# One core: 64 of the dense tokens take their expert activations from gathered rows

## The chip, the cores and the metric

One NeuronCore of a Trainium2 chip runs the whole layer in one launch. The metric is device time in microseconds. The engines are TensorE (PE in the rows, with its weight loads as PEld), VectorE (DVE), ScalarE (ACT), GpSimd (POOL, which here issues the indirect gathers) and SyncE (SP, which issues most loads).

## The reference

One encoder block: adaLN, a mixer, a residual, and then a channel sub-layer that this change is about. In it each token retrieves, for each of 8 heads, 16 of 16,384 single-neuron experts (product keys), and gets their weighted sum:

```python
idx = jnp.take_along_axis(cand_i, best_pos, axis=-1)     # [tokens, 8, 16]
g = jax.nn.softmax(best_s, axis=-1)
u_sel = expert_u[idx]
act = jax.nn.gelu(jnp.einsum('phkd,pd->phk', u_sel, xb), approximate=False)
coef = (g * act.astype(jnp.float32)).astype(xb.dtype)
return jnp.einsum('phk,phkd->pd', coef, expert_v[idx])
```

There are 512 tokens of width 1024; everything is float32.

## The kernel before

The first 128 tokens are **sparse**: for each of their 128 (head, rank) pairs GpSimd gathers one row of `expert_u` per token (`gath`, 128 rows of 4 KB, 0.524 MB a gather), VectorE multiplies it with the token and sums (`dots`, tile `scr`). Later the same is done with `expert_v` (`sums`, tile `ys`). That makes 128 + 128 gathers, each with one VectorE instruction of 128x1024.

The other 384 tokens are **dense**: all 16,384 experts are computed for them as 128 chunks of 128 experts, and a gate tensor `Gd`, zero where a token did not choose an expert, picks out the chosen ones.

After a prologue (norms, mixer, queries, scores) come two stages:

* **Activation stage.** `u_chunk(c)`: 24 matmuls with 384 columns (`mm3`: 8 blocks of the width, three products each of weights and tokens split in a high and a low part), then a Gelu. `split_w` makes the high part on ScalarE (`whi`) and the low part on VectorE (`wlo`), once a chunk. Between chunks a generator, `background_E`, is drawn on: the first top-16 (`stage1`), `topk_tile` for each of four 128-token tiles, and `gates_tile` for the three dense ones. A gate step makes one-hot tiles `jh` and `igh` for four tokens, four float32 matmuls (`ps_gt`) and a copy to `stg`; every fourth step a 1 MB store to `Gd`. What is drawn is set by nominal costs: each chunk adds `STEP_E` to one budget for the background, and `STEP_ED` to one for `dots`. Activations that don't fit the ring of 32 are spilled to `Ad`.
* **Output stage.** `v_chunk`: 18 matmuls with 512 columns into six accumulators. `v_load` brings the weights, every eighth chunk three 512 KB pieces of gates (`gt`), and spilled activations. `v_coef` makes the coefficients: `cf` = activation x gate (VectorE), `ch` its high part (ScalarE), `cl` the rest (VectorE). `cf` has one buffer, `ch` and `cl` three, the split weights four. u chunks that the activation stage had no time for run here too, one beside each v chunk. The sparse work is drawn by a third budget with the factor `F_P`, and what is left after the last chunk is done at once.

The scheduling layer (`tc`) then orders each engine's instructions; each engine runs its own list strictly in order. So does each DMA queue's issuing engine.

Of the kernel before, what the change touches and what calls it, by code (L numbers as in the profile page):

```python
# [8 lines left out]
F32 = mybir.dt.float32  # L9
# [25 lines left out]
def block_kernel(ctx, tc, xT, small, w_ada1, w_ada, b_ada, w_in, w_r, w_i, w_out, w_q, keys, uT, u, v, final_g, out):  # L35
# [11 lines left out]

# [1 line left out]
    small_sb = const.tile([128, NSMALL], F32, name="small_sb")  # L49
# [67 lines left out]

# [1 line left out]
    adx = ExitStack()  # L119
# [150 lines left out]

# [1 line left out]
    mix = mx.enter_context(tc.tile_pool(name="mix", bufs=1))  # L272
# [98 lines left out]

# [1 line left out]
    pst = psA.tile([128, NT], F32, name="ps_col")  # L373
# [17 lines left out]
    nc.vector.scalar_tensor_tensor(A2, adac[:, 32:40], 1.0, sm("n2g"), op0=OP.add, op1=OP.mult)  # L391
    h2n = persist.tile([128, D], F32, name="h2n")

    def full2(k, f):
        if k % 4 == 0:
            tp_cur[0] = psZ.tile([128, 4, 128], F32, name="ps_g", bufs=2)
        nc.tensor.transpose(tp_cur[0][:, k % 4, :], f[:, 0:128], ident)
        if k % 4 == 3:
            nc.scalar.activation(h2n[:, (k - 3) * 128:(k + 1) * 128], tp_cur[0], AF.Copy)

    tp_cur = [None]
    qraw = {0: load_w(w_q[0]), 1: load_w(w_q[1])}
# [4 lines left out]

# [1 line left out]
    ep = ExitStack()  # L409
    sel = ctx.enter_context(tc.tile_pool(name="sel", bufs=1, side="right"))  # L410
    ring = ctx.enter_context(tc.tile_pool(name="ring", bufs=1, side="right"))
# [58 lines left out]

# [84 lines left out]

    def gates_tile(t):
        for gq in range(8):
            stg = stgp[0].tile([128, 128, 16], F32, name="stg", bufs=2)
            for q4 in range(4):
                t0 = gq * 16 + q4 * 4  # L560
                jh = topk.tile([128, 4, 128], F32, name="jh", bufs=2)
                nc.vector.tensor_tensor(jh, iota[:, None, :].to_broadcast([128, 4, 128]),  # L562
                                        selT[t][:, 1, t0:t0 + 4, None].to_broadcast([128, 4, 128]), op=OP.is_equal)
                ig = topk.tile([128, 4, 128], F32, name="igh", bufs=2)
                for k in range(4):
                    col = lambda n: selT[t][:, n, t0 + k:t0 + k + 1]
                    if k < ACT_OH:
# [11 lines left out]
                yield 600 + 236 * (4 - ACT_OH)  # L579

# [21 lines left out]
    def background_E():  # L602
# [15 lines left out]

    def gath(table, idxs, k):
        if k < 128 and k not in rows:  # L620
# [3 lines left out]
            rows[k] = r  # L624

    def dots():
        for k in range(128):
            for kk in range(k, k + (rows_pool[1] - 1 if rows_pool[2] else 1)):
                gath(u, idx_s, kk)
            scr = rows_pool[0].tile([128, D], F16, name="scr")  # L630
            with tc.issue_after(anchor[0]):
                nc.vector.scalar_tensor_tensor(scr, rows.pop(k), 1.0, h2n, op0=OP.mult, op1=OP.mult,  # L632
                                               accum_out=acts[:, k:k + 1])
            yield 1135

    def sums():
        nc.scalar.activation(acts, acts, AF.Gelu)
        nc.vector.tensor_mul(acts, acts, g_s)
        for k in range(128):
            for kk in range(k, k + rows_pool[1] - 1):  # L640
                gath(v, idx_s, kk)
            with tc.issue_after(anchor[0]):
# [5 lines left out]

# [1 line left out]
    hd = lambda k: h2h[:, k, 128:]  # L650
    ld = lambda k: h2l[:, k, 128:]
    uraw = {}
# [11 lines left out]
    act = {}  # L664
    Ad = dram.tile([NE, 128, ND], F32, name="Ad")

# [20 lines left out]
    while not done and c < NE:
        u_load(c + UE + 1)
        u_split(c + UE)
        u_chunk(c, psE, 2)  # L690
        if c >= RB - 4:
            spill(c - RB + 4)
        if sready:
# [4 lines left out]
        while budget > 0:  # L698
# [4 lines left out]
            budget -= n  # L703
        c += 1
    for _ in range(XE):
        u_load(c + UE + 1)
        u_split(c + UE)
        u_chunk(c, psE, 2)
        if c >= RB - 4:
            spill(c - RB + 4)  # L710
        c += 1
    rows_pool[2] = False
# [4 lines left out]

# [1 line left out]
    vp = ctx.enter_context(tc.tile_pool(name="vp", bufs=2, reuse_waits="tile"))  # L719
# [8 lines left out]
    def v_load(n):  # L728
# [95 lines left out]

# [1 line left out]
    x1s = []  # L826
# [92 lines left out]
```

## Time and profile before

| | |
|---|---|
| three runs | 1482.51, 1483.49 (median), 1487.41 us |
| span of the profiled execution | 1481.2 us |
| busy in that span: TensorE, VectorE, ScalarE, GpSimd | 1434.8, 1228.9, 679.6, 303.9 us |
| moved by DMA | 406.51 MB, 274 GB/s over the span |

The span is the time from the first to the last instruction of one profiled execution; the median of the runs lies 2.25 us above it. Busy shares are averages over stages with different limits, so what a change in one stage is worth has to be read in that stage.

### The profile page before, as it was taken

Reading aid. Unit: us, or ns where it says so; the run is one execution under the profiler, and the core shown is the slowest. Engines: PE = TensorE matmul, PEld = TensorE weight load, DVE = VectorE, ACT = ScalarE, POOL = GpSimd, SP = SyncE. Lnnn points to the kernel's source line nnn. Section 1 sums busy time; section 2 is a strip of 40 time slices with the busy share of each in tenths; the row PEclk is TensorE's granted clock in tenths of the full one; section 3 lists DMA queues with packets and bytes.
Section 4 is the critical chain, followed back from the end, with each engine's and each line's share of the span. In section 5 each row is a group of like instructions: output and inputs, shape, how many; then the busy total and the mean of one; then the engine's idle time right before and its main releaser. Section 6 shows DMA issues by size and latency. Waiting matters only on the chain.

```text
span 1481.2 us, 21793 instructions
## 1 busy us (share of the span) xinstructions
PE 1434.8 (97%) x7705; PEld 1256.8 (85%) x7705; DVE 1228.9 (83%) x2501; ACT 679.6 (46%) x1033; POOL 303.9 (21%) x270
## 2 busy tenths in 40 slices
PE   5999998989999999999999999999999999999997
PEld 2666787788999999999999989999888888888885
DVE  6775646999999999978888778788888888888887
ACT  3554434432336567656777633333333333333333
POOL 0000000000133232232222244444222222222200
PEclk9999998999999999999999999999999999999999
DMA  9566231245679988999888799899999999999881
GB/s 383 201 248 213 86 100 57 86 127 146 224 223 366 317 314 305 345 324 326 282 281 285 276 376 347 297 354 323 387 340 366 346 349 337 348 332 320 303 281 57
DMA packets 165312, 406.51 MB, mean 274 GB/s; under 512 B 14674, under 2 KB 84306, under 8 KB 160084
## 3 DMA queue, kind: packets, MB, share of 16 engines
q1 hardware_dynamic: 112724, 227.90, 44.8%
q0 software_dynamic: 37504, 136.33, 25.9%
q10 hardware_dynamic: 14976, 40.90, 7.3%
q8 instruction: 60, 0.98, 0.3%
q14 instruction: 48, 0.39, 0.1%
HBM read 359.99 MB, written 45.09 MB: 273 GB/s over the span
## 4 chain that ended last, share of the span: by engine, by line
PE 66%; DMA 1%; DVE 1%; ACT 0%; issue 0%; DVEq 0%; SPq 0%
PE acc L765 12%; PE acc L769 12%; PE acc L767 12%; PE ps_act L84 8%; PE ps_act L85 8%; PE ps_act L86 8%; PE ps_gt L575 6%; DMA gt<-Gd 1%; DMA Gd<-stg 1%; DVE rows L846 0%; PE acc L777 0%; PE acc L775 0%; PE acc L776 0%; ACT stg L576 0%; DVE rows L839 0%; DVE rows L838 0%
## 5 line engine op out<-in xcount | busy, mean ns | idle before, releaser
L75 ACT ACTIVATE whi<-wraw 128x1024 fp32r<-128x1024 f32 x292 | 307.7, 1054 | 336.9 <-PE ps_act L85 184.5
L76 DVE TENSOR_TENSOR wlo<-wraw,whi 128x1024 fp32r<-128x1024 f32 x292 | 356.3, 1220 | 64.1 <-ACT whi L75 60.2
L86 PE MATMUL ps_act<-h2h,wlo 128*128 128x384 f32 x1024 | 344.7, 337 | 7.8 <-DVE wlo L76 7.8
L84 PE MATMUL ps_act<-h2h,whi 128*128 128x384 f32 x1024 | 349.2, 341 | 1.3 <-ACT sc L465 1.2
L85 PE MATMUL ps_act<-h2l,whi 128*128 128x384 f32 x1024 | 343.1, 335 | 0.0
L622 POOL DMA_INDIRECT rows<-in_u_dram,idx_s x128 | 162.1, 1267 | 451.1 <-DVE scr L632 278.4
L765 PE MATMUL acc<-whi,ch 128*128 128x512 f32 x750 | 231.8, 390 | 3.5 <-ACT ch L756 3.5
L767 PE MATMUL acc<-wlo,ch 128*128 128x512 f32 x750 | 231.8, 390 | 0.0
L769 PE MATMUL acc<-whi,cl 128*128 128x512 f32 x750 | 231.7, 390 | 0.0
L622 POOL DMA_INDIRECT rows<-in_v_dram,idx_s x128 | 136.5, 1067 | 361.4 <-DVE ys L646 337.4
L756 ACT ACTIVATE ch<-cf 128x384 fp32r<-128x384 f32 x128 | 67.1, 525 | 310.6 <-DVE ys L646 234.4
L86 PEld LDWEIGHTS ps_act<-h2h,wlo 128*128 128x128 f32 x1024 | 192.2, 188 | 12.5 <-DVE wlo L76 12.5
L84 PEld LDWEIGHTS ps_act<-h2h,whi 128*128 128x128 f32 x1024 | 192.4, 188 | 3.0 <-ACT sc L465 1.4
L85 PEld LDWEIGHTS ps_act<-h2l,whi 128*128 128x128 f32 x1024 | 192.5, 188 | 0.8
L765 PEld LDWEIGHTS acc<-whi,ch 128*128 128x128 f32 x750 | 140.7, 188 | 31.8 <-ACT ch L756 3.8
L769 PEld LDWEIGHTS acc<-whi,cl 128*128 128x128 f32 x750 | 141.2, 188 | 29.7 <-DVE cl L757 0.3
L767 PEld LDWEIGHTS acc<-wlo,ch 128*128 128x128 f32 x750 | 141.1, 188 | 29.7
L646 DVE SCALAR_TENSOR_TENSOR ys<-rows,acts,ys 128x1024 f32<-128x1024 f32 x127 | 162.6, 1280 | 0.7
L632 DVE SCALAR_TENSOR_TENSOR scr<-rows,h2n 128x1024 f16<-128x1024 f32 x128 | 156.3, 1221 | 3.6 <-DMA rows<-in_u_dram,idx_s 2.9
L757 DVE TENSOR_TENSOR cl<-cf,ch 128x384 fp32r<-128x384 f32 x128 | 71.4, 558 | 88.7 <-ACT ch L756 85.9
L576 ACT ACTIVATE stg<-ps_gt 128x512 f32<-128x512 f32 x96 | 102.3, 1082 | 5.7 <-PE ps_gt L575 3.9
L575 PE MATMUL ps_gt<-igh,jh 128*128 128x128 f32 x768 | 96.0, 275 | 3.1 <-DVE jh L562 3.1
(229 smaller groups left out, 1662.3 us busy)
## 6 DMA issues: line engine op xcount, KB each, us to landing
wraw<-in_uT_dram SPq DMA_DIRECT2D x128, 512.0 KB
wraw<-in_v_dram SPq DMA_DIRECT2D x128, 512.0 KB
Gd<-stg ACTq DMA_DIRECT2D x24, 1024.0 KB
gt<-Gd SPq DMA_DIRECT2D x48, 512.0 KB
wada<-in_w_ada_dram SPq DMA_DIRECT2D x16, 1024.0 KB
Ad<-act ACTq DMA_DIRECT2D x80, 192.0 KB
act<-Ad SPq DMA_DIRECT2D x80, 192.0 KB
wraw<-in_w_in_dram SPq DMA_DIRECT2D x20, 512.0 KB
```

Source lines behind the costliest of these rows:

```text
L75: nc.scalar.activation(hi, raw, AF.Copy)
L76: anchor[0] = nc.vector.tensor_sub(lo, raw, hi.bitcast(F32)).ins
L84: nc.tensor.matmul(ps, hi[:, k, :], xh(k), start=first and k == ks[0], stop=False)
L85: nc.tensor.matmul(ps, hi[:, k, :], xl(k), start=False, stop=False)
L86: nc.tensor.matmul(ps, lo[:, k, :], xh(k), start=False, stop=last and k == ks[-1])
L575: nc.tensor.matmul(pg[:, k, :], jh[:, k, :], ig[:, k, :], start=True, stop=True)
L622: nc.gpsimd.indirect_dma_start(out=r[:, :], out_offset=None, in_=table, in_offset=bass.IndirectOffsetOnAxis(ap=idxs[:, k:k + 1], axis=0))
L632: nc.vector.scalar_tensor_tensor(scr, rows.pop(k), 1.0, h2n, op0=OP.mult, op1=OP.mult, accum_out=acts[:, k:k + 1])
L646: nc.vector.scalar_tensor_tensor(ys, rows.pop(k), acts[:, k:k + 1], ys, op0=OP.mult, op1=OP.add)
L765: nc.tensor.matmul(accs[b][e], ch[:, bs], hi[:, e * 512:(e + 1) * 512], start=st, stop=False)
L767: nc.tensor.matmul(accs[b][e], ch[:, bs], lo[:, e * 512:(e + 1) * 512], start=False, stop=False)
L769: nc.tensor.matmul(accs[b][e], cl[:, bs], hi[:, e * 512:(e + 1) * 512], start=False, stop=en)
```

## The change

Tokens 128 to 191 (the first half of dense tile 1, `XB` = 64) leave the dense activation product: it has 320 columns now. Their activations come from gathered rows, 64 tokens on each half of the partitions, so that 64 gathers and 64 VectorE instructions serve 64 tokens x 128 pairs. The first 64 steps of `dots` are theirs. `coef_b` puts Gelu on these activations, brings them to the layout of the gates with one matmul, and multiplies them into the gates, so that for these tokens `Gd` holds gate x activation. Their 16 gate steps move to the end of the background, and there all four one-hot tiles of a step are made on VectorE, where ScalarE had made one of four. In `v_coef` ScalarE copies those 64 columns from the gates to `cf`, and VectorE multiplies the other 320. `full2` also transposes the 64 tokens (two matmuls a block). The three budgets have new numbers.

```diff
+            for dst, src in zip((h2n, h2b), tp_cur):
+                nc.scalar.activation(dst[:, (k - 3) * 128:(k + 1) * 128], src, AF.Copy)
...
+    NU = ND - XB
...
+            if t == 1:
+                nc.scalar.activation(selB[:, 0:2, :], pt[:, 0:2, 0:XB], AF.Copy)
+                nc.scalar.activation(gTb, pt[:, 2, 0:XB], AF.Copy)
+                nc.vector.scalar_tensor_tensor(ij[:, 0], ij[:, 0], 128.0, ij[:, 1], op0=OP.mult, op1=OP.add)
+                idf = ij[:, 0].rearrange("p h k -> p (h k)")
+                for e in range(2):
+                    nc.vector.tensor_copy(idx_b[XB * e:XB * (e + 1), :], idf[0:XB, XB * e:XB * (e + 1)])
...
+        yield from topk_tile(1)
+        sready.append(1)
         yield from topk_tile(0)
-        sready.append(1)
-        yield from topk_tile(1)
-        yield from merge(gates_tile(1), topk_tile(2), 0.48)
-        yield from merge(gates_tile(2), topk_tile(3), 0.48)
-        yield from gates_tile(3)
+        yield from merge(gates_tile(1, range(4, 8), selT[1]), topk_tile(2), 0.32)
+        yield from merge(gates_tile(2, range(8), selT[2]), topk_tile(3), 0.48)
+        yield from gates_tile(3, range(8), selT[3])
+        while len(bdone) < XB:
+            yield next(dot_gen)
+        coef_b()
+        yield from gates_tile(1, range(4), selB, 0)
...
+    def coef_b():
+        for e in range(2):
+            es = slice(XB * e, XB * (e + 1))
+            nc.scalar.activation(act_p[es, es], act_b[es, :], AF.Gelu)
+        pt = psE.tile([128, 4, 128], F32, name="ps_t")
+        nc.tensor.matmul(pt[:, 0, 0:XB], act_p, sel2, start=True, stop=True)
+        nc.vector.tensor_mul(selB[:, 2, :], pt[:, 0, 0:XB], gTb)
...
+    usteps = [(idx_b, h2b, act_b, k) for k in range(XB)] + [(idx_s, h2n, acts, k) for k in range(128)]
...
-    hd = lambda k: h2h[:, k, 128:]
-    ld = lambda k: h2l[:, k, 128:]
+    hd = lambda k: h2h[:, k, T - NU:]
+    ld = lambda k: h2l[:, k, T - NU:]
...
-        nc.vector.tensor_mul(cf.rearrange("p (g t) -> p g t", t=16),
-                             act.pop(vorder[n]).rearrange("p (g t) -> p g t", t=16), gbuf.pop(n))
+        g = gbuf.pop(n)
+        nb = XB // 16
+        nc.scalar.activation(cf[:, 0:XB].rearrange("p (g t) -> p g t", t=16), g[:, 0:nb], AF.Copy)
+        nc.vector.tensor_mul(cf[:, XB:].rearrange("p (g t) -> p g t", t=16),
+                             act.pop(vorder[n]).rearrange("p (g t) -> p g t", t=16), g[:, nb:])
...
+XB = 64
 ACT_OH = 1
-STEP_E = 2450
-STEP_ED = 1400
+STEP_E = 2070
+STEP_ED = 1180
 GB_E = 4
 GB_P = 7
-F_P = 0.81
+F_P = 0.96
```

The new budgets move instructions on every engine. On TensorE all 128 u chunks now stand in the activation stage (106 before), three of them behind the last gate step (four before); the output stage is 128 v chunks and nothing else. Of the 192 dot products 104 stand in the activation stage (103 of 128 before) and 88 in the output stage, with 96 of the 128 `ys` steps.

ScalarE in the output stage, before (`ch` for one chunk, `whi` for a later one):

```order
L756 ACTIVATE ch_11511<-cf_11509 128x384
L75 ACTIVATE whi_11470<-wraw_11431 128x1024
L756 ACTIVATE ch_11546<-cf_11544 128x384
L75 ACTIVATE whi_11505<-wraw_11466 128x1024
L756 ACTIVATE ch_11585<-cf_11583 128x384
```

and with the change:

```order
L799 ACTIVATE ch_13168<-cf_13165 128x384
L77 ACTIVATE whi_13161<-wraw_13121 128x1024
L794 ACTIVATE cf_13204<-gt_12969 128x64
L799 ACTIVATE ch_13207<-cf_13204 128x384
L794 ACTIVATE cf_13240<-gt_12969 128x64
L77 ACTIVATE whi_13200<-wraw_13157 128x1024
L799 ACTIVATE ch_13243<-cf_13240 128x384
```

The new copy into `cf` stands behind the `whi` of its chunk in 40 chunks, and ahead of it in 81; since `cf` has one buffer, it can't start before the `cl` of the chunk before has read it.

VectorE at the same place, before:

```order
L757 TENSOR_TENSOR cl_11512<-cf_11509,ch_11511 128x384
L752 TENSOR_TENSOR cf_11544<-act_11433,gt_11289 128x384
L76 TENSOR_TENSOR wlo_11471<-wraw_11431,whi_11470 128x1024
L646 SCALAR_TENSOR_TENSOR ys_8675<-rows_11323,acts_2587,ys_8675 128x1024
L757 TENSOR_TENSOR cl_11547<-cf_11544,ch_11546 128x384
```

and with the change:

```order
L800 TENSOR_TENSOR cl_13169<-cf_13165,ch_13168 128x384
L795 TENSOR_TENSOR cf_13204<-act_13084,gt_12969 128x320
L78 TENSOR_TENSOR wlo_13162<-wraw_13121,whi_13161 128x1024
L684 SCALAR_TENSOR_TENSOR ys_9393<-rows_13043,acts_2613,ys_9393 128x1024
L800 TENSOR_TENSOR cl_13208<-cf_13204,ch_13207 128x384
L684 SCALAR_TENSOR_TENSOR ys_9393<-rows_13079,acts_2613,ys_9393 128x1024
L795 TENSOR_TENSOR cf_13240<-act_13123,gt_12969 128x320
L78 TENSOR_TENSOR wlo_13201<-wraw_13157,whi_13200 128x1024
```

A row (`scr` or `ys`) stands between `wlo` and `cl` of nearly every chunk; in 53 chunks a second one stands between `cl` and `cf`.

VectorE at the end of the program, before:

```order
L757 TENSOR_TENSOR cl_13846<-cf_13843,ch_13845 128x384
L752 TENSOR_TENSOR cf_13849<-act_13785,gt_13552 128x384
L757 TENSOR_TENSOR cl_13852<-cf_13849,ch_13851 128x384
L838 TENSOR_TENSOR rows_13908<-acc00_8665,gt_13855 128x512
L839 TENSOR_TENSOR rows_13908<-rows_13908,rows_13862 128x512
```

and with the change (buffer numbers left out, as equal rows then merge):

```order
L795 TENSOR_TENSOR cf<-act,gt 128x320
L684 SCALAR_TENSOR_TENSOR ys<-rows,acts,ys 128x1024
L800 TENSOR_TENSOR cl<-cf,ch 128x384
L684 SCALAR_TENSOR_TENSOR ys<-rows,acts,ys 128x1024 x32
L881 TENSOR_TENSOR rows<-acc_9380,gt 128x512
L881 TENSOR_TENSOR ys<-ys,gt 128x512 x2
```

Now 32 `ys` steps stand between the last coefficients and the closing arithmetic of all four tiles, where there was nothing, and the closing of tile 0 (`ys`) stood further up.

## Rows read from the trace of the kernel before

**Rows 1.** The page, part 1: engines' busy time, share of the span, instructions.
```profile
PE 1434.8 (97%) x7705; PEld 1256.8 (85%) x7705; DVE 1228.9 (83%) x2501; ACT 679.6 (46%) x1033; POOL 303.9 (21%) x270
```

**Rows 2.** The page, part 4: the chain that ended last, by line.
```profile
PE acc L765 12%; PE acc L769 12%; PE acc L767 12%; PE ps_act L84 8%; PE ps_act L85 8%; PE ps_act L86 8%; PE ps_gt L575 6%; DMA gt<-Gd 1%; DMA Gd<-stg 1%; DVE rows L846 0%; PE acc L777 0%; PE acc L775 0%; PE acc L776 0%; ACT stg L576 0%; DVE
```

**Rows 3.** Windows: busy us per engine, PEclk, DMA share, GB/s.
```profile
262.00:423.00 161.00, 152.24 (x873) 139.60 (x872) 160.84 (x764) 59.46 (x85) 8.84 (x10) 1.00 0.47 148
423.00:600.00 177.00, 172.62 (x1079) 171.21 (x1078) 173.72 (x364) 106.50 (x178) 58.75 (x46) 1.00 0.91 317
600.00:840.00 240.00, 240.00 (x1561) 239.97 (x1560) 206.50 (x410) 163.64 (x280) 66.38 (x53) 1.00 0.87 303
840.00:862.00 22.00, 19.09 (x116) 18.77 (x114) 9.68 (x14) 7.61 (x10) 8.72 (x8) 1.00 0.91 314
...
1035.00:1441.00 406.00, 406.00 (x1793) 336.28 (x1792) 337.46 (x394) 147.31 (x199) 83.45 (x88) 1.00 0.96 339
```

**Rows 4.** The chain in order of time: start, us, what.
```profile
829.58 0.89 PE ps_gt L575 x8
834.66 1.78 PE ps_gt L575 x16
```

**Rows 5.** Timeline of VectorE in the activation stage: start, us, what.
```profile
722.71 1.22 DVE L76 TENSOR_TENSOR wlo<-wraw,whi 128x1024 fp32r<-128x1024 f32 x1
723.85 1.22 DVE L632 SCALAR_TENSOR_TENSOR scr<-rows,h2n 128x1024 f16<-128x1024 f32 x1
...
724.99 0.69 DVE L562 TENSOR_TENSOR jh<-iota,selT 128x512 f32<-128x512 f32 x1
725.60 0.95 DVE L572 TENSOR_SCALAR igh<-iota,selT 128x128 f32<-128x128 f32 x3
726.36 0.69 DVE L562 TENSOR_TENSOR jh<-iota,selT 128x512 f32<-128x512 f32 x1
```

**Rows 6.** Timeline in the output stage, one chunk of ScalarE and VectorE.
```profile
1103.72 0.53 ACT L756 ACTIVATE ch<-cf 128x384 fp32r<-128x384 f32 x1 [2.60 <-DVE ys L646]
...
1104.15 1.04 ACT L75 ACTIVATE whi<-wraw 128x1024 fp32r<-128x1024 f32 x1
...
1104.27 0.56 DVE L757 TENSOR_TENSOR cl<-cf,ch 128x384 fp32r<-128x384 f32 x1 [0.60 <-ACT ch L756]
...
1104.87 0.56 DVE L752 TENSOR_TENSOR cf<-act,gt 128x384 f32<-128x384 f32 x1
...
1105.34 1.22 DVE L76 TENSOR_TENSOR wlo<-wraw,whi 128x1024 fp32r<-128x1024 f32 x1
...
1106.48 1.28 DVE L646 SCALAR_TENSOR_TENSOR ys<-rows,acts,ys 128x1024 f32<-128x1024 f32 x1
...
1107.80 0.53 ACT L756 ACTIVATE ch<-cf 128x384 fp32r<-128x384 f32 x1 [2.60 <-DVE ys L646]
```

**Rows 7.** Windows: a stretch of the output stage.
```profile
1040.00:1080.00 40.00, 40.00 (x178) 33.15 (x177) 33.68 (x40) 14.08 (x20) 8.96 (x10) 1.00 1.05 392
```

**Rows 8.** The chain from the last gates to the first coefficients.
```profile
841.93 1.88 ACT stg L576 x2
843.83 7.52 DMA Gd<-stg
851.41 9.91 DMA gt<-Gd
861.44 0.57 DVE cf L752
```

**Rows 9.** Timeline of VectorE: the first dot product of the sparse tokens.
```profile
423.41 1.23 DVE L632 SCALAR_TENSOR_TENSOR scr<-rows,h2n 128x1024 f16<-128x1024 f32 x1
```

**Rows 10.** Timeline of VectorE at the program's end.
```profile
1459.23 0.56 DVE L757 TENSOR_TENSOR cl<-cf,ch 128x384 fp32r<-128x384 f32 x1 [0.85 <-ACT ch L756]
1461.12 0.69 DVE L838 TENSOR_TENSOR rows<-acc,gt 128x512 f32<-128x512 f32 x1 [1.33 <-PE acc L777]
...
1476.81 1.42 DVE L846 SCALAR_TENSOR_TENSOR rows<-rows,rs,gt 128x512 f32<-128x512 f32 x2
```

More of the change, by code (lines that the diff above doesn't have):

```diff
@@ L62, in block_kernel @@
         nc.vector.memset(hind[64 * s:64 * s + 64, s:s + 1], 1.0)
+    sel2 = const.tile([128, XB], F32, name="sel2")
+    nc.vector.tensor_add(sel2, ident[:, 0:XB], ident[:, XB:2 * XB])
     h2h = persist.tile([128, KB, T], FR, name="h2h")
@@ L392, in block_kernel @@
     h2n = persist.tile([128, D], F32, name="h2n")
+    sel = ctx.enter_context(tc.tile_pool(name="sel", bufs=1, side="right"))
+    h2b = sel.tile([128, D], F32, name="h2b")
     def full2(k, f):
         if k % 4 == 0:
-            tp_cur[0] = psZ.tile([128, 4, 128], F32, name="ps_g", bufs=2)
+            tp_cur[:] = [psZ.tile([128, 4, 128], F32, name="ps_g", bufs=2) for _ in range(2)]
         nc.tensor.transpose(tp_cur[0][:, k % 4, :], f[:, 0:128], ident)
+        for e in range(2):
+            nc.tensor.matmul(tp_cur[1][XB * e:XB * (e + 1), k % 4, :], f[:, 128:128 + XB], ident, start=True, stop=True)
         if k % 4 == 3:
-            nc.scalar.activation(h2n[:, (k - 3) * 128:(k + 1) * 128], tp_cur[0], AF.Copy)
-    tp_cur = [None]
+            for dst, src in zip((h2n, h2b), tp_cur):
+                nc.scalar.activation(dst[:, (k - 3) * 128:(k + 1) * 128], src, AF.Copy)
+    tp_cur = []
     qraw = {0: load_w(w_q[0]), 1: load_w(w_q[1])}
@@ L409, in block_kernel @@
     ep = ExitStack()
-    sel = ctx.enter_context(tc.tile_pool(name="sel", bufs=1, side="right"))
     ring = ctx.enter_context(tc.tile_pool(name="ring", bufs=1, side="right"))
@@ L487, in block_kernel @@
     selT = {}
+    idx_b = sel.tile([128, XB], I32, name="idx_b")
+    selB = sel.tile([128, 3, XB], F32, name="selB")
+    gTb = sel.tile([128, XB], F32, name="gTb")
     def topk_tile(t):
@@ L553, in topk_tile, with gates_tile @@
             nc.scalar.activation(selT[t][:, 3:5, :], pt[:, 0:4:2, :], AF.Copy, scale=-1.0)
+            if t == 1:
[5 more added lines that the diff above has]
+                    nc.vector.tensor_copy(idx_b[XB * e:XB * (e + 1), :], idf[0:XB, XB * e:XB * (e + 1)])
         yield 300
-    def gates_tile(t):
-        for gq in range(8):
+    def gates_tile(t, groups, sl, aoh=None):
+        aoh = ACT_OH if aoh is None else aoh
+        for gq in groups:
             stg = stgp[0].tile([128, 128, 16], F32, name="stg", bufs=2)
@@ L578, in gates_tile @@
                     nc.scalar.dma_start(Gd[t][gq], stg)
-                yield 600 + 236 * (4 - ACT_OH)
+                yield 600 + 236 * (4 - aoh)
     stgp = []
@@ L607, in background_E, with gath @@
         stgp.append(ep.enter_context(tc.tile_pool(name="stgp", bufs=1, side="right")))
+        yield from topk_tile(1)
+        sready.append(1)
         yield from topk_tile(0)
-        sready.append(1)
-        yield from topk_tile(1)
-        yield from merge(gates_tile(1), topk_tile(2), 0.48)
-        yield from merge(gates_tile(2), topk_tile(3), 0.48)
-        yield from gates_tile(3)
-    acts = sel.tile([128, 128], F32, name="acts")
+        yield from merge(gates_tile(1, range(4, 8), selT[1]), topk_tile(2), 0.32)
[5 more added lines that the diff above has]
+        yield from gates_tile(1, range(4), selB, 0)
+    acts = sel.tile([128, 128], F32, name="acts")
+    act_b = sel.tile([128, XB], F32, name="act_b")
+    act_p = sel.tile([128, 2 * XB], F32, name="act_p")
+    nc.vector.memset(act_p, 0.0)
+    bdone = []
+    def coef_b():
+        for e in range(2):
+            es = slice(XB * e, XB * (e + 1))
[3 more added lines that the diff above has]
+        nc.vector.tensor_mul(selB[:, 2, :], pt[:, 0, 0:XB], gTb)
     rows = {}
     rows_pool = [topk, GB_E, True]
-    def gath(table, idxs, k):
-        if k < 128 and k not in rows:
+    def gath(table, idxs, k, key):
+        if key not in rows:
             r = rows_pool[0].tile([128, D], F32, name="rows", bufs=rows_pool[1])
@@ L623, in gath @@
                                          in_offset=bass.IndirectOffsetOnAxis(ap=idxs[:, k:k + 1], axis=0))
-            rows[k] = r
+            rows[key] = r
+    usteps = [(idx_b, h2b, act_b, k) for k in range(XB)] + [(idx_s, h2n, acts, k) for k in range(128)]
     def dots():
-        for k in range(128):
-            for kk in range(k, k + (rows_pool[1] - 1 if rows_pool[2] else 1)):
-                gath(u, idx_s, kk)
+        for n, (_, hn, dst, k) in enumerate(usteps):
+            for m in range(n, min(n + (rows_pool[1] - 1 if rows_pool[2] else 1), len(usteps))):
+                gath(u, usteps[m][0], usteps[m][3], m)
             scr = rows_pool[0].tile([128, D], F16, name="scr")
             with tc.issue_after(anchor[0]):
-                nc.vector.scalar_tensor_tensor(scr, rows.pop(k), 1.0, h2n, op0=OP.mult, op1=OP.mult,
-                                               accum_out=acts[:, k:k + 1])
+                nc.vector.scalar_tensor_tensor(scr, rows.pop(n), 1.0, hn, op0=OP.mult, op1=OP.mult,
+                                               accum_out=dst[:, k:k + 1])
+            bdone.append(n)
             yield 1135
@@ L639, in sums @@
         for k in range(128):
-            for kk in range(k, k + rows_pool[1] - 1):
-                gath(v, idx_s, kk)
+            for kk in range(k, min(k + rows_pool[1] - 1, 128)):
+                gath(v, idx_s, kk, kk)
             with tc.issue_after(anchor[0]):
@@ L664, in block_kernel @@
     act = {}
-    Ad = dram.tile([NE, 128, ND], F32, name="Ad")
+    Ad = dram.tile([NE, 128, NU], F32, name="Ad")
     def spill(c):
@@ L672, in u_chunk @@
         hi, lo = usp.pop(c)
-        ps = pool.tile([128, ND], F32, name="ps_act", bufs=bufs)
+        ps = pool.tile([128, NU], F32, name="ps_act", bufs=bufs)
         mm3(ps, hi, lo, hd, ld, range(KB), True, True)
-        act[c] = ring.tile([128, ND], F32, name="act", bufs=RB)
+        act[c] = ring.tile([128, NU], F32, name="act", bufs=RB)
         act_anchor[0] = nc.scalar.activation(act[c], ps, AF.Gelu).ins
@@ L680, in block_kernel @@
     budget = bd_ = 0.0
-    c = 0
     done = False
@@ L686, in block_kernel, with u_step @@
         u_split(j)
[L687 to L692, printed above, removed]
+    def u_step():
+        i = cn[0]
+        u_load(i + UE + 1)
+        u_split(i + UE)
+        u_chunk(i, psE, 2)
+        if i >= RB - 4:
+            spill(i - RB + 4)
+        cn[0] += 1
+    cn = [0]
+    while not done:
+        if cn[0] < NE:
+            u_step()
         if sready:
@@ L703, in block_kernel @@
             budget -= n
-        c += 1
     for _ in range(XE):
[L706 to L711, printed above, removed]
+        if cn[0] < NE:
+            u_step()
+    c = cn[0]
     rows_pool[2] = False
@@ L739, in v_load @@
         if act[cc] is None:
-            act[cc] = ring.tile([128, ND], F32, name="act", bufs=RB)
+            act[cc] = ring.tile([128, NU], F32, name="act", bufs=RB)
             nc.sync.dma_start(act[cc], Ad[cc])
```

6 lines of the change are left out of this document (3 added, 3 removed).

## The prediction

> **What bounds the kernel now.** I began with the page: TensorE is busy 97% of the span, VectorE 83% [rows 1]. The chain that ended last says the same: two thirds of it are matmuls, in thirds of the output product, the u product and the gates [rows 2]. Then windows by stage [rows 3]. Until 423 us VectorE is full (160.84 of 161) and TensorE loses 9. From 423 to 600 both are nearly full (TensorE loses 4.4). From 600 on TensorE has no gap and VectorE 14% of slack, in the output stage 17%. So TensorE sets the time, and the engine right behind it is VectorE; the change takes work from the first and gives work to the second, so I count both, stage by stage. DMA is the third to watch: its share is 0.96 in the output stage.
>
> **Prices.** Between two groups of gate records (829.58 + 0.89 and 834.66) lies one u chunk of 4.19 us [rows 4], 24 matmuls of 384 columns at 0.175 us. An output chunk takes 4.08 us (two `ch` apart, [rows 6]), 18 matmuls of 512 columns at 0.227. So 128 columns cost 0.052 us, 64 half of that: a chunk of 320 columns costs 4.19 - 24 x 0.026 = 3.56. On VectorE the slot of an instruction is the distance of starts in a full stretch [rows 5]: `wlo` 1.14, a dot 1.14, `jh` 0.61, three `igh` 0.76. In the output stage [rows 6] `cl` takes 0.60, `cf` 0.47 (0.40 at 320 columns), `ys` 1.28; in sums over both kinds of row I count 1.17.
>
> **1. The first dot** starts at 423.41 [rows 9]. Ahead of it VectorE now has five more `wlo` (32 for 27; 5.7 us) and one `jh`; some pieces of the four top-k tiles change places, which cancels within 2 us. Between the cast of the indices and the first dot only some 2.4 us of work are left, so it waits for its gather, 0 to 3 us. I take 432. Since VectorE is full up to there, it decides, and TensorE stands at 31 u chunks.
>
> **2. The rest of the activation stage.** TensorE: 97 chunks x 3.56 = 345, 96 gate groups x 0.89 = 85, the small matmul of `coef_b` 1: 431 us. VectorE: it was busy 173.72 + 206.5 + 9.68 = 390 us in the same stretch up to the first `cf` [rows 3]; 15 more `wlo` (17), 16 more `igh` (4) and 4 us of top-k moved make 415, 96% of 431. In the stretch where VectorE stood at 98%, TensorE lost 2.5% [rows 3], so I add 10 us. TensorE is through at 873, and the last gates, with three u chunks behind them, at 862.
>
> **3. The turn.** From the last gates to the first `cf` it takes 861.44 - 841.93 = 19.5 us: two copies, the store of 1 MB, the load of `gt` [rows 8]. The u chunks behind the gates cover 11 of it. First `cf` at 882.
>
> **4. The output stage.** Before, 22 u chunks and 124 output chunks lay between the first `cf` (861.44) and the last `cl` (1459.23, [rows 10]): 22 x 4.19 + 124 x 4.08 = 598, as measured. Now there are 124 output chunks, and three things want about 4.1 us for each. TensorE: 4.08. VectorE with ScalarE: the copy into `cf` can't start before the last `cl`, and where `whi` stands behind it, `wlo` waits for both. By ScalarE's two sizes in rows 6 (0.53 for 384 columns, 1.04 for 1024) a copy of 64 columns takes some 0.27, a slot of 0.24. The three kinds of chunk: `whi` ahead of the copy, 0.46 (what of `whi` outlasts `cl`) + 1.14 + 1.17 + 0.56 = 3.3 us (40 chunks); copy ahead, no row between, 0.24 + 1.04 + 1.14 + 1.17 + 0.58 = 4.2 (25); a second row between `cl` and `cf`, 1.17 + 0.40 + 1.14 + 1.17 + 0.56 = 4.4 (53; 4.5 with `ys`). Their mean is 4.0. DMA: 0.524 MB of weights, 0.197 of gates, 104/128 x 0.164 of spilled activations, 184/128 x 0.524 of rows, 1.61 MB a chunk: 394 GB/s at 4.08 us, where the stage had 339 over 406 us [rows 3]; but over 40 us it had 392, with TensorE at no loss [rows 7]. Buffers are three or four chunks deep, so the slowest mean decides and not the sum of the stalls; I take 4.15: 515 us, last `cl` at 1397.
>
> **5. The end.** 32 `ys` stand behind the last `cl`. TensorE's last three chunks (12 us) hide under them; nothing hides them. At 1.28 they need 41 us; a gather of 0.524 MB in 1.28 us is 409 GB/s, so I take 1.35, 43 us: 1440. The closing of three tiles took from 1461.12 to 1478.2 with some waits for TensorE, and the last store 3 us more [rows 10]; four tiles without those waits, 19.5 + 3: 1462. `full2` has 16 matmuls and two copies more, in a part of the prologue where TensorE waits anyway: 0 to 3.6 us (16 x 0.22, a quarter of a gate group), I take 1.5. That is a span of 1464; with the 2.25 us by which the median stands above the span, **1466 us**.
>
> So the u product gives back 128 x 0.63 = 80 us of TensorE time, and about 63 of it are lost again: 42 to the `ys` at the end, 17 to the first dot, to the fuller VectorE and to the shorter cover at the turn.
>
> **A rule against it.** Rows 7 show 392 GB/s over 40 us. The Trainium skill (DMA: Bandwidth & Descriptors, section Bandwidth, "Where 436 GB/s comes from") says that for transfers between HBM and SBUF the HBM side binds, at about 358 GB/s for a core. By that rule the output stage would need 1.61/358, 4.49 us a chunk. The trace disagrees over 40 us, and over 406 us it shows only that 339 was enough.
>
> **Rivals.**
> *A. DMA holds the output stage.* If what DMA can keep up lies nearer to the 339 GB/s of the whole stage than to 392, say at 358, a chunk takes 4.49: 124 x 0.34 = 42 us, and the `ys` at the end 1.46 each, 4 more: 1512. For it: a share of 0.96 already. Against it: rows 7. (The rule above is this rival.)
> *B. The copy in `v_coef` makes VectorE and ScalarE the bound, and the kernel slower.* If the third kind of chunk sets the pace, or a `whi` comes late now and then, the mean is 4.35: 25 us, 1491. It decides from 4.33 a chunk on, where the sum passes 1488. For it: the order of ScalarE, and VectorE at 96% elsewhere. Against it: 40 chunks keep the old order, and `ch` and `cl` have three buffers.
> *C. All fits.* No loss in the activation stage (10 us less), 4.08 in the output stage (9) and 1.28 a `ys` (2): 1445. For it: from 600 us on TensorE has no gap beside a VectorE at 86%. Against it: VectorE at 96%.
> *D. The matmuls don't get shorter,* because the weight load, busy 239.97 of 240 us beside 384 columns [rows 3], needs those 0.175 us itself. Then the u chunks stay at 4.19: 97 x 0.6 = 58 us more, 1524. Against it: eight gate records, each with a weight load of its own, take 0.89 us, 0.11 each [rows 4].
>
> **How the numbers follow.** Less than 0.3% (4.5 us) can't be told from no change here: 1479 to 1488 is "same". My forecast (1452 to 1480) gets 0.49, A 0.12, B 0.20, C 0.14, D 0.05. Faster: C and nearly all of the forecast, 0.60. Same: the rest of the forecast and somewhat under half of B, 0.12. Slower: what is left of B, A and D, 0.28. The range goes from 1444, below C, to 1504, which leaves out half of A's weight, D and the lower edge of C. For the likeliest case alone it is 1452 to 1480.
>
> **What the profile will show.** `ps_act` matmuls at about 0.149 us from start to start (D: 0.175). The first `scr` at 432, the last `ps_gt` at 862, the first `cf` at 882, the last `cl` at 1397. In the output stage 4.15 us a chunk; if it is more, the wait ahead of `wlo` names `whi` and ScalarE (B), or the wait ahead of `scr` and `ys` names the gathers and GB/s stays under 370 (A). At the end 32 `ys` in a row with TensorE idle for some 30 us. What would make me wrong most is the pace of the output stage: 0.1 us a chunk is 12 us. Next is the activation stage, if VectorE at 96% costs TensorE more than the 2.5% that it cost at 98%.

## The result, and the profile after

The changed kernel takes **1466.84 us** (median of four runs, 1464.85 to 1469.09) against 1483.15 for the kernel before beside it: a ratio of 0.9879, 95% interval 0.9861 to 0.9897. It is faster by 1.2%. The forecast was 1466. Two executions at a much lower granted clock, one of a variant below (0.61) and one of the kernel before (0.85), are left out of every median and ratio.

The profiled execution has a span of 1463.1 us. The page, parts 1 and 4 (busy time and share of each engine, and the chain that ended last), answering to [rows 1, 2]:

```profile
PE 1362.9 (93%) x7739; PEld 1178.7 (81%) x7739; DVE 1283.4 (88%) x2651; ACT 697.0 (48%) x1135; POOL 384.2 (26%) x334
...
PE 45%; issue 23%; POOL 15%; DVE 12%; DMA 3%; ACT 1%; POOLq 0%; SPq 0%; DVEq 0%; ACTq 0%
```

TensorE does 72 us less, VectorE 55 us more. GpSimd has come into the chain: its gathers are the chain's way back from the `ys` at the end (GpSimd itself is busy only 26% of the span).

The windows of the kernel after, cut at its own landmarks (first dot, last gates, first `cf`, last `cl`, last `ys`), answering to [rows 3]; busy us of each engine, then granted clock, DMA share, GB/s:

```profile
262.00:432.00 170.00, 162.15 (x1043) 149.24 (x1042) 167.03 (x790) 71.35 (x112) 8.29 (x11) 0.99 0.46 155
432.00:600.00 168.00, 162.52 (x1126) 161.45 (x1125) 166.53 (x322) 97.32 (x155) 64.08 (x45) 0.98 0.94 338
600.00:858.00 258.00, 258.00 (x1900) 257.88 (x1899) 241.31 (x484) 182.59 (x297) 63.08 (x56) 1.00 0.92 327
858.00:870.00 12.00, 10.31 (x71) 10.04 (x69) 4.10 (x5) 3.88 (x6) 2.26 (x2) 1.00 0.93 322
870.00:1395.00 525.00, 520.67 (x2270) 426.50 (x2271) 479.43 (x654) 218.63 (x383) 217.47 (x189) 0.99 1.02 391
1395.00:1442.00 47.00, 7.98 (x36) 6.27 (x34) 42.02 (x35) 0.00 (x0) 27.66 (x26) 0.62 0.94 355
```

VectorE is full up to the first dot, both engines nearly so until 600 us, then TensorE has no gap until the last gates. In the output stage TensorE is full again, and DMA carries 391 GB/s with a share of 1.02, where it had 339 and 0.96. Then, for 47 us, only `ys` steps run, beside TensorE's last two chunks.

The first dot starts at 432.6, as the group of its tile says (min, median and max ns; first and last start):

```profile
L669 DVE SCALAR_TENSOR_TENSOR scr<-rows,h2b x64: 1210/1221/1237, 432.6 to 675.6; 128x1024 f16<-128x1024 f32 x64
```

The chain around the turn (start, us, what), answering to [rows 8]:

```profile
856.12 0.15 PE ps_act L87
856.27 0.15 PE ps_act L88
...
859.14 7.08 DMA Gd<-stg
866.22 0.02 issue
866.23 3.41 DMA gt<-Gd
```

A `ps_act` matmul now comes every 0.147 us instead of 0.175. The turn is shorter than it was: the `gt` load behind the last `Gd` store takes 3.41 us where it took 9.91. SyncE's queue (issue time, us) shows two of the three loads ahead of the store, which was issued at 859.14:

```profile
855.28 1.01 SPq L776 DMA_DIRECT2D gt<-Gd  x2
...
866.23 0.36 SPq L776 DMA_DIRECT2D gt<-Gd  x1
```

In the kernel before they came behind it; the store was issued at 843.83:

```profile
850.00 4.13 SPq L736 DMA_DIRECT2D gt<-Gd  x3
```

TensorE's start into the output stage:

```profile
871.42 0.79 PE L808 MATMUL acc<-whi,ch 128*128 128x512 f32 x1 [3.12 <-ACT ch L799]
872.69 0.80 PE L808 MATMUL acc<-whi,ch 128*128 128x512 f32 x1 [0.48 <-ACT act L714]
873.29 1.05 PE L810 MATMUL acc<-wlo,ch 128*128 128x512 f32 x2
874.14 1.05 PE L812 MATMUL acc<-whi,cl 128*128 128x512 f32 x2
...
880.38 0.61 PE L808 MATMUL acc<-whi,ch 128*128 128x512 f32 x2
880.84 0.62 PE L810 MATMUL acc<-wlo,ch 128*128 128x512 f32 x2
```

After the gap of 3.12 us two matmuls take 0.85 us from start to start, until 877.55; from 878.5 on they take 0.45. That is the lower of TensorE's two clock levels (1.2 GHz) for some 6 us: the granted clock from 871.4 to 877.5 was 0.50. At the full clock a chunk is 18 x 0.227 = 4.08 us, as before.

VectorE at the end, answering to [rows 10]:

```profile
1395.02 0.56 DVE L800 TENSOR_TENSOR cl<-cf,ch 128x384 fp32r<-128x384 f32 x1
1395.49 38.27 DVE L684 SCALAR_TENSOR_TENSOR ys<-rows,acts,ys 128x1024 f32<-128x1024 f32 x29
1434.26 1.28 DVE L684 SCALAR_TENSOR_TENSOR ys<-rows,acts,ys 128x1024 f32<-128x1024 f32 x1 [0.50 <-DMA rows<-in_v_dram,idx_s]
1437.77 1.28 DVE L684 SCALAR_TENSOR_TENSOR ys<-rows,acts,ys 128x1024 f32<-128x1024 f32 x1 [2.22 <-DMA rows<-in_v_dram,idx_s]
1440.31 1.28 DVE L684 SCALAR_TENSOR_TENSOR ys<-rows,acts,ys 128x1024 f32<-128x1024 f32 x1 [1.26 <-DMA rows<-in_v_dram,idx_s]
```

32 `ys` in 46 us, 1.44 each: 29 come every 1.32 us, and the last three wait 4.0 us for their gathers. TensorE's last matmul starts at 1402.60, 60 us ahead of the end, where it was 10 us before (1470.9 of 1481.2). Most of the time that the shorter matmuls gave back is spent there.

### The profile page after: what moved, and what is told of

It is laid out like the page before. It is cut to its first block, busy times and chain, and to the rows that moved or that the text cites. A ratio compares the mean times of both kernels' runs of the same rounds, so it can differ in the third digit from the quotient of the medians.

```text
span 1463.1 us, 22415 instructions
## 1 busy us (share of the span) xinstructions
PE 1362.9 (93%) x7739; PEld 1178.7 (81%) x7739; DVE 1283.4 (88%) x2651; ACT 697.0 (48%) x1135; POOL 384.2 (26%) x334
## 4 chain that ended last, share of the span: by engine, by line
PE 45%; issue 23%; POOL 15%; DVE 12%; DMA 3%; ACT 1%; POOLq 0%; SPq 0%; DVEq 0%; ACTq 0%
POOL rows L657 15%; PE ps_act L86 7%; PE ps_act L88 7%; PE ps_act L87 7%; PE ps_gt L593 6%; PE ps_z L88 5%; PE ps_z L86 5%; PE ps_z L87 5%; DVE wlo L78 3%; DVE rep L428 1%; PE ps_row L130 1%; DVE scr L669 1%; DMA rows<-in_v_dram,idx_s 1%; DVE ti L430 1%; PE ps_g L467 1%
## 5 line engine op out<-in xcount | busy, mean ns | idle before, releaser
L88 PE MATMUL ps_act<-h2h,wlo 128*128 128x320 f32 x1024 | 319.7, 312 | 8.4 <-DVE wlo L78 7.8
L86 PE MATMUL ps_act<-h2h,whi 128*128 128x320 f32 x1024 | 324.4, 317 | 1.2 <-ACT sc L471 1.2
L87 PE MATMUL ps_act<-h2l,whi 128*128 128x320 f32 x1024 | 318.0, 311 | 0.0
L657 POOL DMA_INDIRECT rows<-in_u_dram,idx_s x128 | 134.0, 1047 | 320.9 <-DVE scr L669 299.3
L657 POOL DMA_INDIRECT rows<-in_v_dram,idx_s x128 | 158.1, 1235 | 161.9 <-DVE ys L684 139.9
L657 POOL DMA_INDIRECT rows<-in_u_dram,idx_b x64 | 87.0, 1359 | 261.5 <-DVE best L426 117.2
L794 ACT ACTIVATE cf<-gt 128x64 f32<-128x64 f32 x128 | 32.6, 255 | 216.5 <-DVE cl L800 212.2
```

Source lines behind the costliest of these rows:

```text
L86: nc.tensor.matmul(ps, hi[:, k, :], xh(k), start=first and k == ks[0], stop=False)
L87: nc.tensor.matmul(ps, hi[:, k, :], xl(k), start=False, stop=False)
L88: nc.tensor.matmul(ps, lo[:, k, :], xh(k), start=False, stop=last and k == ks[-1])
```

## The experiments

What was open after the result: from the first `cf` (870.3) to the last `cl` (1395.0) lie 525 us, 4.23 for each of the 124 chunks that I had put there, where TensorE needs 4.08 and I had taken 4.15. Three theories: **T**, TensorE alone; **V**, the chain between VectorE and ScalarE (rival B); **D**, DMA at a ceiling (rival A, at another price). And each term of the sum was to be priced alone. All ratios are to the kernel before on the same chip (its medians lay between 1485.0 and 1486.5 there); the changed kernel stands at 0.9879.

### The u product keeps its width

```diff
-    hd = lambda k: h2h[:, k, T - NU:]
+    hd = lambda k: h2h[:, k, T - ND:]
...
-        act_anchor[0] = nc.scalar.activation(act[c], ps, AF.Gelu).ins
+        act_anchor[0] = nc.scalar.activation(act[c], ps[:, XB:], AF.Gelu).ins
```

> The changed kernel, but the u product keeps its 384 columns (the Gelu takes the last 320 of them). If the shorter matmuls are what gives the time back, 97 chunks behind the first dot cost 97 x 0.65 = 63 us more, and the 31 ahead of it (20 us more on TensorE, which has some 8 us of gaps there) some 10: about +73, 1540 us. If the gain comes from elsewhere (the new budgets, the order of the background), the time stays under 1490. ps_act matmuls at 0.175 us from start to start, the output stage as it was (4.23 us a chunk).

Measured: 1540.15 us, ratio 1.0364 (1.0329 to 1.0399), 0.0485 or 72 us above the changed kernel. Its windows, in the same columns, show where:

```profile
432.00:600.00 168.00, 168.00 (x1021) 167.93 (x1020) 154.64 (x293) 86.49 (x142) 57.49 (x42) 1.00 0.86 300
600.00:840.00 240.00, 240.00 (x1537) 240.00 (x1536) 187.88 (x365) 152.13 (x263) 49.10 (x48) 1.00 0.87 294
```

TensorE has no gap, and VectorE falls to 78% for want of something to do. The price of the columns is right, and the added rows without shorter matmuls would have made the kernel 3.6% slower than before.

### The added rows left out

```diff
+        yield from topk_tile(0)
+        sready.append(1)
         yield from topk_tile(1)
-        sready.append(1)
-        yield from topk_tile(0)
...
+    nc.vector.memset(act_b, 0.0)
-    usteps = [(idx_b, h2b, act_b, k) for k in range(XB)] + [(idx_s, h2n, acts, k) for k in range(128)]
+    usteps = [(idx_s, h2n, acts, k) for k in range(128)]
```

> The changed kernel without the 64 added rows: the activations of the 64 tokens are zeros instead of the gathered dot products, and the first dots are those of the sparse tokens (tile 0's top-k goes first again). 152 sparse steps remain for the output stage where 184 fit, so no ys stands behind the last cl: 42 us less at the end, of which some 8 come back because TensorE's last three chunks are no longer covered; 8 us less at the first dot, 3 in the output stage's last chunks. About 1466 - 45 = 1421 us. That is the price of the added rows by the prediction's terms. If the rows cost only VectorE slack, under 15 us less.

Measured: 1411.54 us, 0.9503 (0.9462 to 0.9544), 56 us below the changed kernel. TensorE's last matmul starts at 1397.79, only 5 us earlier; the program ends 10 us behind it instead of 60. So the rows cost 56 us, nearly all of it behind TensorE's end. I had said 45: the closing of tile 0, which waits for the last `ys`, hides under TensorE's last chunks once there is no tail, and that I had not counted (argued from the two ends, not tried by itself).

### Two buffers for `cf`

```diff
-        cf = vp.tile([128, ND], F32, name="cf", bufs=1)
+        cf = vp.tile([128, ND], F32, name="cf", bufs=2)
```

> The changed kernel with two buffers for cf instead of one, so that ScalarE's copy no longer waits for the cl before it. Theory V (the chain of copy, whi, wlo between ScalarE and VectorE makes the output stage 4.23 us a chunk instead of 4.08): the wait of that copy goes, and the stage falls to about 4.10, 16 us less, 1450 us. Theory D (DMA at its ceiling of some 400 GB/s) and theory T (TensorE with small losses): unchanged within 4 us, 1466, and a wait elsewhere takes its place.

Measured: 1472.97 us, 0.9918 (0.9892 to 0.9944): not faster, at the edge of slower. From the first `cf` (873.9) to the last `cl` (1398.05) it takes 524 us, as before. ScalarE's waits in the output stage, of the changed kernel (us in total, times, longest):

```profile
ACT cf L794 <- DVE cl L800: 211.4, 107, 2.5
...
ACT whi L77 <- DMA wraw<-in_v_dram: 35.2, 23, 3.8
```

and with two buffers:

```profile
ACT cf L794 <- DVE cl L800: 175.8, 85, 8.7
ACT whi L77 <- DMA wraw<-in_v_dram: 107.2, 44, 6.1
```

ScalarE gets further ahead and then waits for the weights instead. The copy's wait shrinks by 36 us and the stage stays as long as it was, which speaks against V; but most of that wait is still there, so this run alone doesn't rule V out. The runs below do.

### The gates loaded once

```diff
-        if n % 8 == 0:
+        if n == 0:
...
-            for k in range(8):
-                gbuf[n + k] = gt[:, :, k, :]
+            for k in range(NE):
+                gbuf[k] = gt[:, :, k % 8, :]
```

> The changed kernel with the gates loaded once (for the first eight chunks) and used for all chunks, so the output is another: 0.197 of 1.61 MB a chunk less by DMA. Theory D: 1.41 MB at the same 400 GB/s would need 3.5 us, so TensorE's 4.08 sets the pace: 18 us less, 1448 us. Theory V: 4.23 us a chunk as before, 1466. In both the ys at the end may go a little faster, by 1 or 2 us, if DMA held them.

Measured: 1467.72 us, 0.9877 (0.9844 to 0.9910): unchanged, though DMA moves 50 GB/s less. The stretch 900 to 1300 us of the changed kernel, and below it that of this one:

```profile
900.00:1300.00 400.00, 398.45 (x1750) 327.16 (x1749) 364.75 (x510) 167.46 (x292) 154.85 (x140) 1.00 1.04 402
```

```profile
900.00:1300.00 400.00, 395.63 (x1733) 326.06 (x1733) 371.93 (x521) 166.88 (x294) 163.28 (x142) 0.99 0.97 352
```

So D falls for the pace of the changed kernel. V doesn't fit either, as TensorE is busy 398.45 and 395.63 of 400 us, and T is left. The mistake was in my count. TensorE's first output matmul starts at 871.42, its last ends at 1403, 532 us for 128 chunks that need 522. The last `cl` comes two chunks ahead of TensorE's end (8 us) and not three (12 us), which is what the prediction's step 5 took over from the kernel before: VectorE has less of a lead. So 126 chunks lie between `cf` and `cl`, 514 us, and 10 are lost: 3 at the lower clock, 3 in five waits of 0.3 to 1.3 us, 1 between the first `cf` and the first matmul, the rest in smaller ones that the trace doesn't name.

### Room for the 32 `ys` in the output stage

`F_P` 1.05 instead of 0.96, alone and with the gates loaded once.

```diff
-F_P = 0.96
+F_P = 1.05
```

> The changed kernel with F_P 1.05 instead of 0.96, so that the 32 ys behind the last cl are drawn inside the output stage. Theory T (TensorE alone sets the stage; VectorE has some 45 us of real slack there): the stage stays as it is, the tail goes, and the closing of tile 0 hides under TensorE's last chunks: 1425 us. Theory V (VectorE's waits for ScalarE can't be filled): the stage grows by what the tail loses, 4.4 us a chunk: 1463 to 1470. Theory D (DMA can't go over some 403 GB/s): 1.74 MB a chunk at 403 is 4.32 us, 28 us more in the stage, 45 to 50 less behind it: 1445 to 1450.

> F_P 1.05, and the gates loaded once (for the first eight chunks) and used for all, so the output is another: 0.197 MB a chunk less. Theory D: DMA now has room (1.55 MB a chunk, 378 GB/s at 4.095 us) and the time falls well below that of F_P 1.05 alone, to 1425 us. Theory V: as F_P 1.05 alone, 1463 to 1470. Theory T: as F_P 1.05 alone, 1425.

Measured: 1460.68 us, 0.9812 (0.9795 to 0.9830), and with the gates loaded once 1420.78 us, 0.9543 (0.9518 to 0.9569). By itself the first number lies nearer to V's forecast than to D's, 11 us above it; the second decides: 40 us (by the ratios) hang on the gates' loads, so D holds here and V doesn't. 900 to 1300 us with `F_P` 1.05:

```profile
900.00:1300.00 400.00, 378.81 (x1592) 299.55 (x1591) 361.90 (x500) 155.76 (x268) 207.40 (x155) 0.98 1.04 403
```

and with the gates loaded once:

```profile
900.00:1300.00 400.00, 394.31 (x1727) 325.02 (x1726) 393.63 (x540) 169.16 (x288) 275.04 (x168) 0.99 1.01 390
```

At 403 GB/s this mix draws no more: VectorE does no more than before (361.90 for 364.75), TensorE runs 9% fewer matmuls (1592 for 1750), and what it waits for is `ch`, 26.0 us in 15 waits. On the way to that `ch` ScalarE waits with `whi` for weights that haven't landed; in the output stage with `F_P` 1.05 (us in total, times, longest), where the changed kernel has 35.2 us in 23 waits:

```profile
ACT whi L77 <- DMA wraw<-in_v_dram: 85.6, 46, 6.1
```

and with the gates loaded once:

```profile
ACT whi L77 <- DMA wraw<-in_v_dram: 0.9, 1, 0.9
```

Without the gates' loads VectorE is busy 393.63 of 400 and the 32 `ys` fit. So neither VectorE nor ScalarE kept them out: DMA did. The changed kernel stands at the edge of that ceiling (402 GB/s). With `F_P` 1.05 TensorE's output product takes 577 us from start to end, 45 more than in the changed kernel, and the time behind the last `cl` falls from 68 to 20, so that hardly anything is won. One rival is open: that the weights come late not by the total rate but because the gates' loads stand ahead of them on SyncE's queue. Loading the gates once takes away both.

### One size, and one-hot tiles on ScalarE

32 tokens instead of 64 (`XB` 32; the two halves of the partitions become four quarters), with budgets between the old and the new, and 0.40 for 0.32 as the share in which the first gates are mixed with `topk_tile(2)`:

```diff
...
-STEP_E = 2070
-STEP_ED = 1180
+STEP_E = 2260
+STEP_ED = 1290
...
-XB = 64
+XB = 32
```

> One size changed: 32 tokens instead of 64 get their activations from gathered rows (32 gathers of 32 tokens x 4 pairs; the u product has 352 columns; STEP_E 2260, STEP_ED 1290, between the old and the new). By the prediction's prices the u product costs 97 x 0.32 = 31 us more behind the first dot, but 189 sparse steps fit the output stage and 11 u chunks' cover stands there, so no ys are left behind the last cl: 50 us less at the end. 1466 - 50 + 31 = 1447 us. If the price of the rows lies in the activation stage and not in the tail: above 1460.

Measured: 1492.77 us, 1.0048 (1.0028 to 1.0069): 46 above the forecast and slower than before. No `ys` is left at the end, as expected, but from TensorE's first output matmul (876.34) to its last (1478) it takes 602 us for 128 x 4.08 + 11 x 3.86 = 565 us of matmuls: 37 us are lost (3.86 lies midway between the prices at 320 and 384 columns; the slot of 0.159 us in this run's trace makes it 3.82), at 382 GB/s and a DMA share of 1.04 (900 to 1300 us).

Two of four one-hot tiles on ScalarE instead of one, and more dots in the activation stage:

```diff
-ACT_OH = 1
+ACT_OH = 2
...
-STEP_ED = 1180
+STEP_ED = 1400
```

> The changed kernel with two instead of one of four one-hot tiles of a gate step made on ScalarE (ACT_OH 2) and STEP_ED 1400: VectorE is relieved of some 80 x 0.25 = 20 us in the activation stage, takes 8 dots more there, and 8 u chunks move to the output stage, where they make room for the 32 ys. TensorE's work is the same. If the tail is only a matter of where VectorE has room: tail gone, 45 to 50 us less, 4 more at the first acc since fewer u chunks cover it: 1420 to 1425 us. If ScalarE, in order and with two instructions for each one-hot tile, holds whi back: TensorE gets gaps in the activation stage and 1440 to 1466 remain.

Measured: 1470.20 us, 0.9879 (0.9840 to 0.9917). The tail is gone, and the time is lost elsewhere. TensorE's longest wait is this one, at the first output matmul (total, times, longest of the group):

```profile
PE acc L808 <- ACT ch L799: 30.1, 4, 17.9
```

The u chunks that moved to the output stage no longer cover the turn, which is longer besides: the `gt` load behind the last store takes 16.14 us, where the changed kernel has 3.41.

```profile
861.76 16.14 DMA gt<-Gd
```

From 432 to 840 us TensorE is busy 389.89 of 408, where the changed kernel has 402.52. That is the second theory's gaps in the activation stage, though the waits don't name `whi` (6.3 us are for `wlo`, 4.4 and 3.3 for one-hot tiles, 3.9 for ScalarE's Gelu); the larger loss is the turn, which I had put at 4 us, and the time lies 4 us above that theory's range. And with the rows of the 32 `ys` inside the output stage, DMA moves 399 GB/s there at a share of 1.03 (900 to 1300 us), again near the ceiling.

### Another layout of the gate tensor

If the ceiling is a matter of packets, the gates are its worst part: a `gt` load reads 512 B pieces. In another layout each partition reads 4 KB in one piece, and the store writes the small pieces instead.

```diff
-    Gd = {t: dram.tile([8, 128, 128, 16], F32, name=f"Gd{t}") for t in range(1, NT)}
+    Gd = {t: dram.tile([128, 16, 8, 128], F32, name=f"Gd{t}") for t in range(1, NT)}
...
-                    nc.scalar.dma_start(Gd[t][gq], stg)
+                    nc.scalar.dma_start(Gd[t][:, :, gq, :], stg.rearrange("p (a i) t -> p a (i t)", a=16))
...
-                nc.sync.dma_start(gt[:, 8 * t - 8:8 * t], Gd[t][:, :, cc:cc + 8, :].rearrange("g j i t -> j g i t"))
+                nc.sync.dma_start(gt[:, 8 * t - 8:8 * t].rearrange("p g i t -> p g (i t)"), Gd[t][:, cc // 8])
```

> F_P 1.05 as before, and another layout of Gd: a gt load reads 4 KB in one piece on each partition instead of eight pieces of 512 B, and the store writes pieces of 512 B instead of whole 8 KB. As many bytes as F_P 1.05 alone (1460.7 us), but fewer packets in the output stage. If the DMA ceiling that F_P 1.05 ran into is a matter of packets (small ones move fewer bytes in their time), the stage gets shorter: up to the 40 us that loading the gates once gave is the bound, some 20 us likely, 1440 us, with GB/s above 404. If the ceiling is one of bytes (402 to 404 GB/s whatever the packets), the time stays at 1458 to 1464, or above by what the scattered store costs.

> The same layout of Gd with F_P 0.96 as in the changed kernel, where TensorE set the output stage. Theory T for that stage: nothing to win there, 1466 us within 4; the store in pieces of 512 B makes the activation stage or the turn up to 10 us longer. If DMA held the changed kernel's stage too, below 1460.

Measured: with `F_P` 1.05 1451.02 us, 0.9765 (0.9731 to 0.9799); with 0.96 1466.01 us, 0.9870 (0.9832 to 0.9908). The layout alone changes nothing in the time of the changed kernel, as T says; where DMA is the bound it gives 7 us by the ratios (10 by the medians), less than half of what I had thought likely, and the two intervals just meet. Both are net of what the scattered store costs: it takes 10.3 to 10.4 us at the turn instead of 6.1 to 7.1, and the first `cf` comes 3 to 4 us later. From the first `cf` to the last `cl` the layout gives 14 us with `F_P` 1.05 (554.5 for 568.7) and 3 with 0.96 (521.6 for 524.7). Packets and rate from 900 to 1300 us with `F_P` 1.05, old layout:

```profile
DMA packets 83402, 161.25 MB, mean 403 GB/s; under 512 B 5981, under 2 KB 52198, under 8 KB 83375
```

and new layout:

```profile
DMA packets 54818, 165.04 MB, mean 413 GB/s; under 512 B 6093, under 2 KB 18448, under 8 KB 54789
```

Fewer packets, 2.5% more bytes a second.

> The other layout of Gd with F_P 1.0: 17 of the 32 ys move into the output stage, 15 stay behind it. At F_P 0.96 TensorE had no gap there (1466), at 1.05 the stage was some 34 us longer for 32 more rows (1451). If DMA, once full, takes 1.27 us a row (0.524 MB at 411 GB/s) and some 6 rows still fit free, the stage grows by 14 us and 24 go at the end: 1453 to 1458. If the stage has room for all 17: 1442.

> 32 tokens from gathered rows (1492.8 us) with the other layout of Gd. There TensorE lost 35 us in the output stage while DMA moved 383 GB/s with a share of 1.05. If that was DMA, held by small packets, the stage gets shorter as it did with 64 tokens and F_P 1.05 (10 us), at most by the 35: 1458 to 1484 us. If the cause is the order on ScalarE and VectorE: unchanged within 4 us.

Measured: `F_P` 1.0 with the new layout 1452.38 us, 0.9773 (0.9755 to 0.9791), a hair better than expected and no different from 1.05. These two versions beat both kernels, the changed one by some 16 us. With 32 tokens the new layout gives 1470.19 us, 0.9901 (0.9880 to 0.9923), 22 us less than the old one: there too DMA held the stage. Its rate rose from 382 to 402 GB/s, with a share of 1.03. Why 32 tokens get fewer bytes a second than 64 at the same share (382 against 403, 402 against 413) stays open; their mix of transfers differs, with 11 u chunks in the stage.

## Why the prediction was right

**Prices.** The slot of a 320-column matmul was 0.147 us where I had taken 0.149; 0.175 at 384 columns and 0.227 in the output product stayed. Rival D is out by the rows, and the wide u product shows the same as a whole: 72 us where the prices give 73.

**1, the first dot:** 432.6 for 432.

**2, the activation stage:** the last gates start at 857.5 for 862, 4.5 early. Up to 600 us TensorE lost 5.5 us, VectorE being full; after that nothing, at a VectorE of 94%. My 10 us of loss were 5 too many.

**3, the turn:** 12 us for 19.5, both from the last copies to `stg`. The mechanism was right (copy, store, load), but its price was taken from a row with a `gt` load of 9.91 us; now it is 3.41, with the other two loads issued ahead of the last store. In the variants that keep this order and have the load on the chain it takes 3.3 to 5.6 us; where two loads are issued behind the store it takes 7.0 (32 tokens, old layout) and 16.1 (two one-hot tiles on ScalarE), and 9.9 in the kernel before. Whether the order on SyncE alone does it wasn't tried. So the first `cf` came 12 us earlier than predicted, 870.3 for 882.

**4, the output stage:** 525 us for 515, so that the last `cl` came at 1395.0 for 1397. The mechanism was right, TensorE sets the pace with DMA and VectorE close behind, but the term was mis-sized: the stall between the engines that I had spread over every chunk (0.07 us each) is nearly absent; instead there are two more chunks between the two landmarks, since VectorE's lead shrank, and 10 us of start and waits. Steps 2 and 3 were early by 4.5 and 7.5 us and step 4 late by 10. That they cancel to 2 us at the last `cl`, and to 1 in the span, is luck; what was sound is that each step was within 10 us.

**5, the end:** 32 `ys` at 1.44 for 1.35 us, 46 for 43; the closing 21.5 for 22.5. Span 1463.1 for 1464. Two smaller slips don't move the sum: the chain in rows 2 is 36% output product, 24% u product and 6% gates, not thirds, and of the 63 us that the prediction says are lost again, the parts it names (42 and 17) make 59.

**The rule against it.** The changed kernel moves 402 GB/s over 400 us, and 413 with the other layout. So the 358 GB/s of the Trainium skill (DMA: Bandwidth & Descriptors, section Bandwidth, "Where 436 GB/s comes from") isn't the limit for this one core; the trace disagrees. The Trainium skill (Perfetto Trace Analysis, section Roofline) also says that a core running alone can pull more than that share; with that the trace agrees. That small packets move fewer bytes, since each has a fixed cost, is in the Trainium skill too (DMA: Bandwidth & Descriptors, section Bandwidth, "Why small descriptors are slow (HBM only)"); 403 against 413 agrees with it in direction.

**Rivals.** A had the right engine and the wrong price: a ceiling is there, at 403 GB/s for this mix, and it decides only when more rows are drawn. The 394 that I had worked out is a mean over the stage (391 measured); from 900 to 1300 us, where more spilled activations come back, TensorE's pace already draws 402. B is out: with the gates' loads gone VectorE and ScalarE carry all rows with TensorE busy 394 of 400 us. Of C the 4.08 us a chunk came true, and half of its 10 us in the activation stage; its 1.28 us a `ys` did not.

**Net.** By the runs the shorter product gives 72 us and the rows cost 56, each found by taking one of the two out of the changed kernel; that leaves 16, and measured are 16 to 18.

## What to carry to other kernels

Trading TensorE columns for gathered rows paid here as far as DMA could bring the rows: count the bytes a chunk against the rate that this mix of packets reaches, before counting engines. When a stage stands just below a second limit, an experiment that relieves only one limit shows nothing (the gates loaded once, and the new layout, were worth 0 alone); push the load up first, and then relieve. And work that is pushed behind the last matmul costs its own time and, as argued above, part of the closing behind it.

## What was not expected of the hardware

DMA held 402 GB/s for 400 us with TensorE full, and 414 with the new layout and `F_P` 1.0, in fewer and larger packets. After a gap of 3 us at the turn, which followed a stretch of 12 us with TensorE busy for 10.31, matmuls ran at the lower level for some 6 us (the granted clock was 0.66 from 870 to 880 us), 3 us of loss beside the gap itself. With `F_P` 1.05 the same happens inside the output stage: after a wait of 3.29 us, which ended at 912.19, two matmuls take 0.85 us from start to start until 915.66, and the granted clock is 0.86 from 910 to 922 us. So a wait of TensorE cost more there than its own length. At the end, with TensorE busy 7.98 of 47 us, it was 0.62, which costs nothing there.
